# An encoder block on one core: the order of work at the start, and when the first MLP results are squared

## The chip, the cores and the metric

The kernel runs on one core of a Trainium2 chip. Its time is the device time of one execution in microseconds (us). TensorE (PE in the profile) multiplies matrices, VectorE (DVE), ScalarE (ACT) and GpSimd (POOL) do elementwise work, SyncE (SP) issues most DMA transfers. Each engine takes its instructions in the order in which the program lists them.

## The reference, cut to what matters

One layer of an encoder over 1024 tokens of width 1024, everything in float32:

```
u = rms_norm(x, norm1_g);  q,k,v,cb,cc,ch,ga,gb = split(u @ w_in)
y_a = neighbourhood_attention(rms_norm(q), rms_norm(k), v) @ w_attn_branch
y_b = (cb * conv3(cc * ch)) @ w_conv_branch
x = x + (sigmoid(ga) * y_a + sigmoid(gb) * y_b) @ w_o
x = x + square(relu(rms_norm(x, norm2_g) @ w_mlp_in)) @ w_mlp_out
```

## The kernel before, in words

Every float32 operand of a product is scaled by a power of two and split into two float16 halves, high and low: ScalarE writes the high half (a scaled copy), then VectorE the low half (scaled value less high half). A product is three passes over the halves. One call of `unit` is one group of matmuls into one PSUM bank; the work that follows it (`post`) and the background generators (`fg`, `bg`) are advanced by `step` and `tick` behind each unit, and that fixes where their instructions stand in each engine's queue. Nothing is reordered at run time. PSUM has eight banks under three names, d and s with three each, o with two.

**The start.** `ln_step` advances the normalisation of one of eight row blocks of 128 tokens (`norm`): a square with a row sum on ScalarE, five small VectorE steps (`rstd`), then `u` in two halves (L421 on ScalarE, L423 on VectorE). Blocks 0 to 2 are turned by TensorE (`ln_trans`), blocks 3 to 7 by DMA transposes from SP's queue (`ln_turn`, L438) into `uT`. `v_unit` makes V, first in units of 256 columns (blocks 0 to 2, each of the two halves of V's weights), then 512 columns for blocks 3 to 7; then come eight units of Q and eight of K. A weight chunk (`Chunk.prep`) needs a scale for the whole chunk, from a bound on its largest value: V's chunks use the largest absolute value (`largest`, L302 on VectorE), Q, K and others the sum of squares (L241 on ScalarE), summed over the partitions by a matmul with ones (`all_sum`, L179). Then the splits: L291 on ScalarE, L278 on VectorE; for the second piece of each V chunk GpSimd makes the low half (L288 and L276). The weights come by DMA from SP's queue (L210), five pieces ahead.

`sforms` makes sums and differences of row blocks n and n+4 of the normalised `x` for the gates, whose products are later made with seven instead of eight block products: two scaled copies on ScalarE (L475), four additions on GpSimd into a buffer `sform` (L481), a split on ScalarE and VectorE (L483, L485), and a store to DRAM from SP's queue (L490). `SFORM` holds the unit from which each of the four pairs starts. After the fourth Q unit the program needs all four to be stored, since `xt` is given up there.

**The first MLP product.** It has 16 blocks (`quad`) of seven units each. The results of a block lie in a tile `as` with seven slots; two such tiles take turns. `h_done` follows a block: ReLU and square on ScalarE (L1432, L1434, the square also gives the sum from which the next scale comes), four additions (`sums`, L1159, on VectorE for blocks 0 and 1, then on GpSimd), and a store to DRAM (L1438). Blocks 0 and 1 are computed in two halves of 256 columns: 0 first half, 1 first half, 0 second half, 1 second half; after them come whole blocks of 512. Meanwhile the next weights are prepared: row scales (L952), sums of squares (L961), sums of blocks on GpSimd (`tsum`, L966), the column of sums (L932, L933), the matmul with ones, the scale (L182 to L412) and the splits (L981 on ScalarE, L977 on VectorE).

Of the kernel before, what the change touches and what calls it, by code (L numbers as in the profile page):

```python
# [52 lines left out]
def encoder_block(ctx: ExitStack, tc: tile.TileContext, x, weights, cols, gqk, rel, masks, out):  # L53
# [63 lines left out]
    fg, bg = [], []  # L117
# [102 lines left out]
    class Chunk:  # L220


        def __init__(self, kind, widths, tag, rows, half, more):
            self.kind, self.bank = kind, {"V": "o", "Q": "o", "K": "s", "C": "d"}.get(kind)
            self.tag, self.rows, self.widths, self.more = tag, rows, widths, more
            self.offs = []
            self.raw, self.ready, self.half, self.pool = [], more > 0, half, () if half is None else (1,)
            self.split = False

        def prep(self):  # L230
# [4 lines left out]
            tot = sum(k * w for k, w in self.widths)  # L235
            if self.kind in "QKCG":
                self.parts = wsp.tile([128, 2, tot], F16, name="w16_ws", tag="ws")
                for p, (k, w) in enumerate(self.widths):
# [7 lines left out]
                V.tensor_tensor(c, sc[:, a], sc[:, gm2], op=OP.mult)  # L246
                yield from apart(units[0], 2 if self.kind == "Q" else 3)
                yield from all_sum(c, b, bank(self.bank) if self.bank else anybank(), 1e-36)
                yield from pow2_half(b, 14, s, self.inv, more=self.more)
# [19 lines left out]
            prev, scaled = None, {}  # L269
            for it in todo + [None]:  # L270
                if prev:
                    p, parts, f = prev
                    for o, m, c in parts:
                        hi, lo = (self.parts[:, w, f + o:f + o + m] for w in range(2))
                        if p in self.pool:
                            G.tensor_tensor(lo, scaled[p][:, o:o + m], hi, op=OP.subtract)  # L276
                        else:
                            V.scalar_tensor_tensor(lo, self.raw[p][:, o:o + m], sc[:, c:c + 1], hi,  # L278
                                                   op0=OP.mult, op1=OP.subtract)
                    done[0] += 1  # L280
                    load_upto(done[0] + 5)
                splitting[0] = True
                if it:
                    p, parts, f = it
                    if p in self.pool:
                        scaled[p] = w1p.tile([128, 1024], F32, name="scaled", bufs=1)
                        for o, m, c in parts:
                            G.tensor_scalar(scaled[p][:, o:o + m], self.raw[p][:, o:o + m], sc[:, c:c + 1], 1.0,  # L288
                                            op0=OP.mult, op1=OP.mult)
                    for o, m, c in parts:  # L290
                        A.activation(self.parts[:, 0, f + o:f + o + m], self.raw[p][:, o:o + m], AF.Copy,  # L291
                                     scale=sc[:, c:c + 1])
# [172 lines left out]
    turned, formed = [0], [0]  # L465
    SFORM = (6, 8, 10, 12)

    def sforms():

        for n, start in enumerate(SFORM):  # L470
            yield from apart(start, 0)
            assert turned[0] >= n + 5
            z = []
            for b in (n, n + 4):
                A.activation(xt[:, b], xt[:, b], AF.Copy, scale=sc[:, at(ys, b)])  # L475
                z += [xt[:, b, :512], xt[:, b, 512:]]
            f = wqk.tile([128, 4, 512], F32, name="sform", bufs=1)
            v = wqk.tile([128, 4, 2, 512], F16, name="s16", bufs=2)
            for o, a, b, op in ((2, z[0], z[2], OP.subtract), (0, z[2], z[3], OP.subtract),
                                (1, f[:, 0], z[0], OP.subtract), (3, z[1], f[:, 1], OP.add)):  # L480
                G.tensor_tensor(f[:, o], a, b, op=op)  # L481
            yield from apart(start, 2)
            A.activation(v[:, :, 0], f, AF.Copy)  # L483
            yield
            V.tensor_tensor(v[:, :, 1], f, v[:, :, 0], op=OP.subtract)  # L485
            fg.append(sform_store(n, v))

    def sform_store(n, v):
        yield from apart(units[0], 1)
        SP.dma_start(GS[:, n], v)  # L490
        formed[0] = n + 1
# [23 lines left out]
    push(cV[0])  # L515
    ln_step(0, 2)
    tick()
    ln_step(0, 5)
    ln_step(1)
# [10 lines left out]
    tick(1)  # L530
    v_unit(0, 0, 0, 0)
    ln_step(2, 4)
    ln_trans(u16[:, 1], 1, UT)
    ln_step(2, 1)
    tick(3)
    ln_step(2)
    tick(4)
    ln_step(3, 2)
    ln_trans(u16[:, 2], 2, UT)
    ln_step(3, 4)  # L540
    fg.append(qk_gain())
    fg.append(sforms())
    V.tensor_reduce(sc[:, gm2], sc[:, g1], axis=AX, op=OP.max, apply_absolute_value=True)
    mul(gm2, gm2, gm2)
    for p in range(11):
        if p == 3:
            flush()
            push(cQ)
        if 0 < p < 6:
            v_unit(p % 3, p // 3, 1, 2)  # L550
        elif p:
            v_unit(p - 3, None, 2, 4)
        for q in (p,) if p < 6 else (2 * p - 6, 2 * p - 5):
# [5 lines left out]
            if c < 7:  # L559
                ln_step(c + 1, 3)  # L560
    settle()
    flush()
# [48 lines left out]
    for n, (kind, b) in enumerate(todo):  # L611
# [309 lines left out]
    def turn_s(i, f):  # L921
        for n in range(4):
            for s in range(2):
                SP.dma_start_transpose(FORM[f](s)[:, :, 128 * n:128 * n + 128], GS[:, n, i, s])

# [264 lines left out]

    spare = []

# [90 lines left out]
    def forms_m():  # L1283
# [10 lines left out]
        t2 = w4p.tile([128, 2, 512], F16, name="t2", bufs=1)  # L1294
        t4 = w4p.tile([128, 2, 512], F16, name="t4", bufs=1)
        k4 = lambda v: v.rearrange("p (k c) -> p k c", k=4)
        flat = {0: lambda i: P1[0][:, 7, i], 1: lambda i: two[:, 0, i], 2: lambda i: two[:, 1, i],
# [128 lines left out]
    AS, live = {}, set()  # L1426
    bsum, R = [keep(4) for _ in range(4)], [(keep(), keep()) for _ in range(4)]
    r_ready = [False] * 4

    def h_done(q):  # L1430
        f = AS.pop(q)
        A.activation(f[:, 0:4], f[:, 0:4], AF.Relu)  # L1432
        yield
        A.activation(f[:, 0:4], f[:, 0:4], AF.Square, scale=sc[:, c1[q].inv],  # L1434
                     accum_out=sc[:, at(bsum[q // 4], q % 4)])
        yield
        yield from sums(f, G if q > 1 else V)
        SP.dma_start(HS[q // 4][:, :, q % 4], f)  # L1438
# [8 lines left out]
    def quad(q, c0=0, c1=512):  # L1447
# [6 lines left out]
        ps = {}  # L1454
        z = [AS[q][:, i, c0:c1] for i in range(7)]

        def post6(ps):
# [281 lines left out]
```

## Time and profile before

| | us |
|---|---|
| median of 3 runs | 1243.88 (1243.17 to 1244.32) |
| the profiled execution | 1241.45 |
| its span in the profile | 1239.7 |
| TensorE busy | 1200.9 |
| VectorE busy | 930.0 |
| ScalarE busy | 765.2 |
| GpSimd busy | 425.5 |

A row of the order of time gives the start and the duration in us, the engine, the line of the kernel, the operation, the tiles written and read, and in brackets how long the engine was idle before it and what ended that. A row by stage gives the busy time of each engine in that stretch and the granted TensorE clock (1.00 is full).

### The profile page before, as it was taken

The numbers are of one execution on the slowest core, as the hardware profiler recorded it, in microseconds if no ns is written. First come the engines' busy times: TensorE is split into PE (matmuls) and PEld (weight loads), VectorE is DVE, ScalarE is ACT, GpSimd is POOL, SyncE is SP. The second block draws the span as 40 slices with busy tenths as digits, with TensorE's granted clock in tenths as the row PEclk, the third lists the DMA queues.
The fourth block names the chain that finished last, engine by engine and source line by source line (L and its number), as shares of the span: only waits on it lengthen the run. The fifth ranks groups of instructions, "written<-read, shape, count | busy, mean of one in ns | idle before, by whom it ended". The sixth has DMA issues, their size and how long they took to land.

```text
span 1239.7 us, 17066 instructions
## 1 busy us (share of the span) xinstructions
PE 1200.9 (97%) x6294; PEld 575.6 (46%) x6294; DVE 930.0 (75%) x1743; ACT 765.2 (62%) x1179; POOL 425.5 (34%) x289
## 2 busy tenths in 40 slices
PE   5989999999999999999999899999999999999998
PEld 3534444444444444444458344444444444444444
DVE  6668677988557777877877654564546999999997
ACT  6777577787474554536767877877765763645430
POOL 2440003111331111101003356556657473473562
PEclk8999999999999999999999999999999999999999
DMA  6557446656651211216096543553474744436202
GB/s 257 107 203 170 79 120 137 133 119 120 132 144 44 68 45 58 68 34 255 18 178 146 204 150 130 187 171 136 161 288 161 300 167 148 167 116 232 102 34 102
DMA packets 170868, 173.36 MB, mean 140 GB/s; under 512 B 131488, under 2 KB 132000, under 8 KB 166688
## 3 DMA queue, kind: packets, MB, share of 16 engines
q1 hardware_dynamic: 170784, 172.27, 47.0%
q8 instruction: 49, 0.80, 0.3%
q14 instruction: 35, 0.29, 0.1%
HBM read 102.51 MB, written 37.75 MB: 113 GB/s over the span
## 4 chain that ended last, share of the span: by engine, by line
PE 67%; DVE 18%; ACT 7%; issue 4%; DMA 1%; POOL 1%; SPq 0%; DVEq 0%; ACTq 0%; POOLq 0%
PE ps_d L188 26%; PE ps_s L188 20%; PE ps_o L188 18%; PE ps_d L859 3%; DVE sz L797 2%; DVE P L823 2%; DVE w_s L977 2%; DVE w_ws L278 1%; DVE ops L1572 1%; POOL sform L481 1%; DMA raw<-in_weights 1%; ACT w_ws L241 1%; ACT as L1432 1%; DVE sc L302 1%; DVE sg L1093 1%
## 5 line engine op out<-in xcount | busy, mean ns | idle before, releaser
L188 PEld LDWEIGHTS <-ops 128*128 128x128 f16 x1356 | 132.4, 98 | 159.5 <-issue 2.7
L188 PEld LDWEIGHTS <-w 128*128 128x128 f16 x1368 | 133.2, 98 | 145.7 <-issue 7.2
L859 PE MATMUL ps_d<-uT,w_ws 128*128 128x512 f16 x528 | 125.4, 379 | 0.0
L188 PE MATMUL ps_d<-ops 128*128 128x512 f16 (+1 forms) x528 | 118.4, 374 | 0.0
L188 PE MATMUL ps_s<-ops 128*128 128x512 f16 x492 | 113.2, 379 | 1.5 <-DVE ops L1572 1.1
L1563 ACT ACTIVATE ops<-hf,sc 128x2048 f16<-128x2048 f32 x26 | 52.0, 1998 | 93.7 <-PE ps_o L188 34.8
L966 POOL TENSOR_TENSOR tsum<-raw 128x512 f32<-128x512 f32 x28 | 45.5, 1637 | 156.5 <-ACT raw L952 145.8
L188 PEld LDWEIGHTS <-uT 128*128 128x128 f16 x648 | 65.0, 101 | 70.4 <-issue 5.6
L1159 POOL TENSOR_TENSOR as<-as 128x512 f32<-128x512 f32 x56 | 76.6, 1369 | 37.1 <-ACT as L1434 33.8
L188 PEld LDWEIGHTS <-w_s 128*128 128x128 f16 x588 | 56.8, 98 | 69.4 <-DVE w_s L977 1.9
L188 PE MATMUL ps_d<-u2x,w 128*128 128x512 f16 (+1 forms) x360 | 80.0, 372 | 0.0
L1565 DVE SCALAR_TENSOR_TENSOR ops<-hf,sc,ops 128x2048 f16<-128x2048 f32 x26 | 74.2, 2852 | 5.2 <-ACT ops L1563 5.2
L188 PE MATMUL ps_o<-ops 128*128 128x512 f16 x336 | 77.1, 379 | 0.0
L859 PEld LDWEIGHTS <-w_ws 128*128 128x128 f16 x528 | 50.8, 98 | 52.5
L188 PE MATMUL ps_o<-u2T,w 128*128 128x512 f16 (+1 forms) x324 | 71.7, 371 | 0.0
L952 ACT ACTIVATE raw<-raw,sc 128x256 f32<-128x256 f32 x172 | 70.8, 493 | 0.7 <-DMA raw<-in_weights 0.7
L966 POOL TENSOR_TENSOR gsum<-raw 128x512 f32<-128x512 f32 x14 | 18.9, 1371 | 131.7 <-issue 57.1
L981 ACT ACTIVATE w<-raw,sc 128x512 f16<-128x512 f32 (+1 forms) x28 | 24.6, 927 | 61.2 <-DVE sc L411 61.2
L188 PE MATMUL ps_s<-u2T,w 128*128 128x512 f16 (+1 forms) x252 | 54.2, 366 | 2.4 <-DVE as L1467 2.4
L1458 DVE TENSOR_TENSOR as<-ps_d,as 128x512 f32<-128x512 f32 (+1 forms) x15 | 10.1, 673 | 58.8 <-ACT as L1475 58.8
L806 ACT ACTIVATE sz<-sz,sc 128x384 f32<-128x384 f32 (+1 forms) x64 | 37.3, 582 | 26.9 <-DVE sc L797 13.5
L278 DVE SCALAR_TENSOR_TENSOR w_ws<-raw,sc,w_ws 128x512 f16<-128x512 f32 (+2 forms) x72 | 46.1, 690 | 2.4 <-ACT w_ws L291 2.4
(336 smaller groups left out, 2615.2 us busy)
## 6 DMA issues: line engine op xcount, KB each, us to landing
raw<-in_weights SPq DMA_DIRECT2D x89, 512.0 KB, 5.5
hs<-as SPq DMA_DIRECT2D x16, 1792.0 KB, 8.7
hf<-hs SPq DMA_DIRECT2D x26, 1024.0 KB, 6.5
w2x<-in_weights SPq DMA_DIRECT2D x16, 512.0 KB, 8.1
raw<-in_weights SPq DMA_DIRECT2D x16, 384.0 KB, 3.8
xt<-in_x SPq DMA_DIRECT2D x8, 512.0 KB, 9.9
gs<-s SPq DMA_DIRECT2D x4, 1024.0 KB, 6.2
x<-in_x SPq DMA_DIRECT2D x8, 512.0 KB, 10.0
```

The lines of the kernel that those rows point to most:

```text
L188: T.matmul(ps, l, r, start=a, stop=b)
L278: V.scalar_tensor_tensor(lo, self.raw[p][:, o:o + m], sc[:, c:c + 1], hi, op0=OP.mult, op1=OP.subtract)
L797: V.tensor_tensor_reduce(z[:, :d["n"]], d["ps"][:, :d["n"]], bm, sc[:, cneg], 3.0e38, OP.add, OP.min, accum_out=sc[:, d["mx"]])
L806: A.activation(z, z, AF.Exp, scale=-1.0, bias=sc[:, d["mx"]], accum_out=sc[:, d["sm"]])
L823: V.scalar_tensor_tensor(d["lo"], d["z"][:, :d["n"]], sc[:, d["r"]], d["hi"], op0=OP.mult, op1=OP.subtract)
L859: T.matmul(ps, l, r, start=a, stop=b)
L952: A.activation(v, v, AF.Copy, scale=sc[:, at(g, 4 * i + k)])
L966: G.tensor_tensor(t[:, o], a, b, op=OP.add)
L977: V.scalar_tensor_tensor(o(1), w, sc[:, s], o(0), op0=OP.mult, op1=OP.subtract)
L1159: sub.tensor_tensor(z[o], z[a], z[b], op=op)
L1563: A.activation(P[:, 1, 0], hf, AF.Copy, scale=sc[:, Rs])
L1565: V.scalar_tensor_tensor(P[:, 1, 1], hf, sc[:, Rs], P[:, 1, 0], op0=OP.mult, op1=OP.subtract)
```

## The change

At the start:

- Row block 1's scale steps stand ahead of the split of V's first weights, and V's first unit of block 1 stands on TensorE ahead of the transposes of block 2 (before, the other way round).
- V's second weight chunk takes its scale from sums of squares on ScalarE instead of maxima on VectorE. All low halves of V's weights are made by VectorE, none by GpSimd.
- On SP's queue the last two of Q's and K's first weight loads stand ahead of the transpose of block 3; before, that transpose stood between them.
- The gates' sums are made in place in `xt`, and each pair is started and split at its own marks (`SFORM`: mark, pair, 0 for the sums or 1 for the split). The split of the first pair stands behind `u` of block 7 on ScalarE; before it stood ahead. The stores leave from ScalarE's queue. The order of the four sums in DRAM changes, and `turn_s` reads them accordingly.
- Q's weights: their scale and splits are advanced earlier, by more ticks and steps in the loop over V's units. K's weights: six instead of three ticks behind the units 5 to 7 of Q, so scale and splits stand one unit earlier.

In the MLP:

- Block 0's first half is squared and summed by itself, before its second half is computed; its second half and block 1 wait some steps. The four sums of blocks 0 and 1 are issued without steps in between.
- Block 2's slots 4 and 5 for intermediate results lie in two buffers that are free by then (`t2`, `t4`), not in the `as` tile that block 0 still stores from.

```diff
-            if self.kind in "QKCG":
-                self.parts = wsp.tile([128, 2, tot], F16, name="w16_ws", tag="ws")
+            if self.kind in "QKCG" or self.half:
+                self.parts = vhome[0][:, 1] if self.half else wsp.tile([128, 2, tot], F16, name="w16_ws", tag="ws")
...
-                        if p in self.pool:
-                            G.tensor_tensor(lo, scaled[p][:, o:o + m], hi, op=OP.subtract)
-                        else:
-                            V.scalar_tensor_tensor(lo, self.raw[p][:, o:o + m], sc[:, c:c + 1], hi,
-                                                   op0=OP.mult, op1=OP.subtract)
+                        V.scalar_tensor_tensor(lo, self.raw[p][:, o:o + m], sc[:, c:c + 1], hi,
+                                               op0=OP.mult, op1=OP.subtract)
...
-    SFORM = (6, 8, 10, 12)
+    SFORM = ((6, 0, 0), (7, 1, 0), (8, 0, 1), (10, 2, 0), (10, 1, 1), (11, 3, 0), (14, 2, 1), (15, 3, 1))
...
+        for mark, n, split in SFORM:
+            yield from apart(mark, 0)
+            pair = xt[:, n:n + 5:4]
+            if not split:
+                for b in (n, n + 4):
+                    A.activation(xt[:, b], xt[:, b], AF.Copy, scale=sc[:, at(ys, b)])
+                z = [xt[:, b, c:c + 512] for b in (n, n + 4) for c in (0, 512)]
+                for o, a, b, op in ((3, 2, 3, OP.subtract), (2, 0, 2, OP.subtract),
+                                    (0, 3, 0, OP.subtract), (1, 1, 0, OP.add)):
+                    G.tensor_tensor(z[o], z[a], z[b], op=op)
+                continue
...
-        SP.dma_start(GS[:, n], v)
+        A.dma_start(GS[:, n], v)
...
     push(cV[0])
-    ln_step(0, 2)
+    ln_step(0, 7)
     tick()
-    ln_step(0, 5)
...
+    ln_step(1, 4)
+    V.tensor_reduce(sc[:, gm2], sc[:, g1], axis=AX, op=OP.max, apply_absolute_value=True)
+    mul(gm2, gm2, gm2)
     flush()
-    ln_step(1, 5)
+    ln_step(1)
...
-        unit(tok_mms(ps, actU, b, ch, 8, 512, 0), post, 4, 3)
+        unit(tok_mms(ps, actU, b, ch, 8, 512, 0), post, 4, 6 if 4 < n < 8 else 3)
...
-    def h_done(q):
-        f = AS.pop(q)
-        A.activation(f[:, 0:4], f[:, 0:4], AF.Relu)
+    def h_done(q, c0=0, c1=512, wait1=0, wait2=0):
+        f = AS[q] if c1 < 512 else AS.pop(q)
+        v = f[:, :, c0:c1]
+        yield from wait(wait1)
+        A.activation(v[:, 0:4], v[:, 0:4], AF.Relu)
...
+        yield from wait(wait2)
+        if q > 1:
+            yield from sums(v, G)
+        else:
+            for _ in sums(v, V):
+                pass
+        if c1 < 512:
+            return
...
         z = [AS[q][:, i, c0:c1] for i in range(7)]
+        if q == 2:
+            z[4:6] = extra
...
-            if c1 == 512:
-                fg.append(h_done(q))
+            if q == 0:
+                fg.append(h_done(q, c0, c1, 3, 4 if c0 else 24))
+            elif c1 == 512:
+                fg.append(h_done(q, 0, c1, *((2, 6) if q == 1 else ())))
```

More of the change, by code (lines that the diff above doesn't have):

```diff
@@ L226, in __init__ @@
             self.offs = []
-            self.raw, self.ready, self.half, self.pool = [], more > 0, half, () if half is None else (1,)
+            self.raw, self.ready, self.half = [], more > 0, half
             self.split = False
@@ L246, in prep @@
                 V.tensor_tensor(c, sc[:, a], sc[:, gm2], op=OP.mult)
-                yield from apart(units[0], 2 if self.kind == "Q" else 3)
-                yield from all_sum(c, b, bank(self.bank) if self.bank else anybank(), 1e-36)
+                if not self.half:
+                    yield from apart(units[0], 2 if self.kind == "Q" else 3)
+                yield from all_sum(c, b, bank(self.bank) if self.bank else anybank(), 1e-36, not self.half)
                 yield from pow2_half(b, 14, s, self.inv, more=self.more)
@@ L268, in prep @@
                 o += k
-            prev, scaled = None, {}
+            prev = None
             for it in todo + [None]:
@@ L529, in encoder_block @@
     push(cV[1])
-    tick(1)
+    tick(2)
     v_unit(0, 0, 0, 0)
@@ L534, in encoder_block @@
     ln_step(2, 1)
-    tick(3)
+    tick(1)
+    v_unit(1, 0, 0, 0)
+    tick(7)
     ln_step(2)
-    tick(4)
-    ln_step(3, 2)
+    ln_step(3, 1)
     ln_trans(u16[:, 2], 2, UT)
-    ln_step(3, 4)
+    tick(2)
+    ln_step(3, 5)
     fg.append(qk_gain())
     fg.append(sforms())
-    V.tensor_reduce(sc[:, gm2], sc[:, g1], axis=AX, op=OP.max, apply_absolute_value=True)
-    mul(gm2, gm2, gm2)
     for p in range(11):
@@ L548, in encoder_block @@
             push(cQ)
-        if 0 < p < 6:
+        if p == 1:
+            step()
+            tick(2)
+        elif p and p < 6:
             v_unit(p % 3, p // 3, 1, 2)
-        elif p:
-            v_unit(p - 3, None, 2, 4)
+        elif p > 5:
+            v_unit(p - 3, None, 0, 4 if p < 7 else 8)
         for q in (p,) if p < 6 else (2 * p - 6, 2 * p - 5):
@@ L560, in encoder_block @@
                 ln_step(c + 1, 3)
+        if p > 5:
+            step(2)
     settle()
@@ L1189, in encoder_block @@
     PART = ((0, 4), (4, 7))
-    spare = []
+    spare, extra = [], []
     def pieces(n, part):
@@ L1295, in forms_m @@
         t4 = w4p.tile([128, 2, 512], F16, name="t4", bufs=1)
+        extra.extend(t.rearrange("p a c -> p (a c)").bitcast(F32) for t in (t2, t4))
         k4 = lambda v: v.rearrange("p (k c) -> p k c", k=4)
```

36 lines of the change are left out of this document (11 added, 25 removed).

## The prediction

> **What bounds the kernel now.** I read the page first, then busy time by stage, then the order of time in the two stretches that the change touches.
>
> ```profile
> span 1239.7 us, 17066 instructions
> ...
> PE 1200.9 (97%) x6294; PEld 575.6 (46%) x6294; DVE 930.0 (75%) x1743; ACT 765.2 (62%) x1179; POOL 425.5 (34%) x289
> ...
> hs<-as SPq DMA_DIRECT2D x16, 1792.0 KB, 8.7
> ...
> gs<-s SPq DMA_DIRECT2D x4, 1024.0 KB, 6.2
> ```
>
> TensorE is busy 1200.9 of 1239.7 us, so no change that leaves its matmuls alone can bring more than the 38.8 us in which it idles, plus what it runs below full clock. By stage (columns: length, then busy time of PE, PEld, DVE, ACT, POOL, granted clock):
>
> ```profile
> 62.00:79.00 17.00, 11.84 (x53) 5.01 (x53) 12.37 (x14) 14.31 (x18) 7.97 (x6) 1.00 0.50 162
> 79.00:170.00 91.00, 91.00 (x427) 41.46 (x426) 67.65 (x191) 57.49 (x104) 6.86 (x6) 1.00 0.64 150
> ...
> 675.00:700.00 25.00, 20.63 (x125) 12.29 (x124) 14.11 (x31) 18.15 (x26) 7.64 (x6) 0.93 0.35 116
> 700.00:900.00 200.00, 200.00 (x938) 90.73 (x936) 110.18 (x229) 149.57 (x220) 119.67 (x88) 1.00 0.49 162
> ```
>
> Two holes lie inside the change's reach: 5.2 us at 62 to 79 (the last unit of V and the first of Q) and 4.4 us at 675 to 700 (the third unit of the MLP). Behind each TensorE is 100% busy (79 to 170, 700 to 900) while VectorE has 26% and 45% to spare: what is won in either hole is not eaten at once.
>
> The first hole in order of time (start, duration, engine, line, and in brackets the idle time before and what ended it):
>
> ```profile
> 12.78 2.46 DVE L278 SCALAR_TENSOR_TENSOR w_v<-raw,sc,w_v 128x256 f16<-128x256 f32 x4
> 14.29 2.73 POOL L276 TENSOR_TENSOR w_v<-scaled,w_v 128x256 f16<-128x256 f32 x4 [0.15 <-ACT w_v L291]
> ...
> 25.84 4.48 PE L188 MATMUL ps_s<-w_v,uT 128*128 128x256 f16 x24
> 27.93 1.15 ACT L421 ACTIVATE u<-xt,sc 128x1024 f16<-128x1024 f32 x1 [1.04 <-DVE sc L400]
> 29.11 1.28 DVE L423 SCALAR_TENSOR_TENSOR u<-xt,sc,u 128x1024 f16<-128x1024 f32 x1 [0.95 <-ACT u L421]
> 30.42 2.11 SPq L438 DMA_TRANSPOSE uT<-u  x1
> 31.47 1.67 DVE L278 SCALAR_TENSOR_TENSOR w_v<-raw,sc,w_v 128x256 f16<-128x256 f32 x4
> 37.39 1.05 ACT L241 ACTIVATE w_ws<-raw 128x1024 bf16<-128x1024 f32 x1
> 41.17 5.34 PE L188 MATMUL ps_s<-w_v,uT 128*128 128x512 f16 x24
> 57.26 1.13 ACT L421 ACTIVATE u<-xt,sc 128x1024 f16<-128x1024 f32 x1
> 62.09 0.99 SPq L490 DMA_DIRECT2D gs<-s  x1
> 64.43 5.35 PE L188 MATMUL ps_s<-w_v,uT 128*128 128x512 f16 x24 [2.35 <-DMA uT<-u]
> 68.34 2.56 ACT L291 ACTIVATE w_ws<-raw,sc 128x512 f16<-128x512 f32 x4 [0.42 <-DVE sc L253]
> 69.62 0.38 PE L188 MATMUL ps_d<-w_ws,uT 128*128 128x512 f16 x1
> 72.33 5.48 DVE L278 SCALAR_TENSOR_TENSOR w_ws<-raw,sc,w_ws 128x512 f16<-128x512 f32 x6
> 78.30 5.34 PE L188 MATMUL ps_o<-w_ws,uT 128*128 128x512 f16 x24
> 81.81 0.67 ACT L578 ACTIVATE qs<-ps_d,sc 128x512 f32<-128x512 f32 x1
> ...
> DMA to landing us min/median/max: 4.2/4.3/5.5
> ```
>
> The last V unit waits until 64.43 for the DMA transpose of row block 7, whose `u` ScalarE wrote only at 57.26. The first Q unit takes 69.62 to 78.30, 8.7 us for 24 matmuls that need 5.18 (a full unit's 5.34 less the overlap with the next one), since Q's low halves appear one by one beside it.
>
> **The change, part by part.** Start. The first scale still needs its second weight piece by DMA, so TensorE's first product stays where it is. V's first half: eight low halves on VectorE instead of four there and four on POOL. Beside POOL four took 2.46; with POOL idle (31.47) 1.67, 0.42 each. Eight come to 3.3 us behind about 1.1 us of small steps that now go first, done near 17.4 against POOL's 17.02. That is covered: TensorE at half clock needs about as long.
>
> V's second half: its scale comes from two sums of squares on ScalarE (1.17 each in sequence, estimated from the 1.05 row and its read-out) instead of two reductions on VectorE. ScalarE has them by about 21.5, one uT copy behind them by 22.5, and the second product of TensorE, now moved ahead of block 2's transposes, starts there instead of at 25.84. The next starts near 29.4, and V's second half has its eight low halves by 32.05. With three units of 2.6 us the first 512-wide unit could start at 39.8 instead of 41.17.
>
> But the row blocks fall back. Block 3's scale now stands behind those eight splits on VectorE, and on SP's queue its transpose stands behind four weight loads instead of two. Step by step with 1.15 (`u`), 1.28 (its low half), the squares, and the copies of VT between, the transposes leave at about 35.85 (before: 30.42), 39.85, 48.4 (behind Q's four sums of squares on ScalarE), 54.3 and 60.0; block 7's `u` is at 57.5, as the splitting of the gates' sums and its wait for POOL no longer stand ahead of it, which repays the delay. With 4.3 to landing: 40.1, 44.1, 52.7, 58.6, 64.3. The units of 5.18 then start at 40.1, 45.4, 52.7 (a gap of 2.1), 58.6 (0.7) and 64.3 (0.5). So the last V unit starts where it did, and the gain there is 0.1.
>
> Q's scale is then read by VectorE at about 64 and the splits run from 65 (before: 68.34). At 0.69 to 0.91 each (72.33: six in 5.48 beside POOL) the eight low halves are done at 72.5; TensorE, from 69.5 on, wants the last at 74.0. So Q's first unit takes its plain 5.18 and ends at 74.7 instead of 78.46. **Begin: -3.8.** Bounds: +0 (the last transpose 3.8 later) and -5.3 (no gaps; then the low halves at 72.5 hold the unit to 73.1).
>
> The new gap of 2.1 may cost clock. Ahead of 64.43 a gap of 2.35 cost none; ahead of 690.39 (below) one of 2.36 was followed by units of 4.23 and 3.00 where 2.75 is usual, 1.7 lost. If the gap at 52.7 costs that, the units after it run to 64.8 and the sum loses 0.5, since they waited for transposes anyway. [...]
>
> The gates' sums in place (same four POOL adds per pair, no extra buffer), later: covered by the stretch 79 to 170. Stores on ScalarE's queue: SP's issue took 0.99, so four cost ScalarE about 4 us and free SP. By my count Q's first result is read at about 81.8, as before (81.81), now 7.1 us after its unit ends instead of 3.4; with two and three PSUM buffers taking turns, a unit waits only when this exceeds 15.5 (three more units). ScalarE has 33 us to spare up to 170. K's scale in one go: K's splits come one unit earlier in program order; covered.
>
> MLP. The second hole:
>
> ```profile
> 665.05 1.76 ACT L981 ACTIVATE w<-raw,sc 128x512 f16<-128x512 f32 x2 [4.44 <-DVE sc L411]
> ...
> 675.30 1.89 ACT L1432 ACTIVATE as<-as 128x2048 f32<-128x2048 f32 x1
> 677.22 2.00 ACT L1434 ACTIVATE as<-as,sc 128x2048 f32<-128x2048 f32 x1
> 677.42 0.17 PE L179 MATMUL ps_d<-ones 128*128 128x1 bf16 x1
> ...
> 679.23 0.36 ACT L1475 ACTIVATE as<-ps_o 128x256 f32<-128x256 f32 x1
> 679.35 1.42 DVE L1159 TENSOR_TENSOR as<-as 128x512 f32<-128x512 f32 x2 [3.58 <-ACT as L1434]
> ...
> 683.28 1.76 ACT L981 ACTIVATE w<-raw,sc 128x512 f16<-128x512 f32 x2 [3.70 <-DVE sc L411]
> ...
> 686.28 2.47 DVE L977 SCALAR_TENSOR_TENSOR w<-tsum,sc,w 128x1024 f16<-128x1024 f32 x2
> 688.80 1.27 POOL L966 TENSOR_TENSOR tsum<-raw 128x512 f32<-128x512 f32 x1 [10.64 <-DVE w L977]
> 689.91 0.42 DVE L1467 TENSOR_TENSOR as<-ps_s,as 128x256 f32<-128x256 f32 x1
> 690.39 4.23 PE L188 MATMUL ps_s<-u2T,w 128*128 128x512 f16 x12 [2.36 <-DVE as L1467]
> ...
> 694.41 3.00 PE L188 MATMUL ps_d<-u2T,w 128*128 128x512 f16 x12
> 699.21 0.16 DVE L933 CAST ones<-sc 128x1 bf16<-128x1 f32 x1
> 699.42 0.16 PE L179 MATMUL ps_s<-ones 128*128 128x1 bf16 x1 [2.01 <-DVE ones L933]
> ```
>
> ScalarE squares block 0's whole result (1.89 + 2.00) ahead of the copy at 679.23, VectorE's in-order queue waits 3.58 for it, the next weights' scale follows only at 683.28, their low halves end at 688.7, and only then does VectorE read the banks that TensorE wants at 688.0. Now half of those squares run around 661, in the 4.44 us that ScalarE waits ahead of 665.05, and the other half stands behind the copy, which comes at 675.4. The scale is then free at 678.6 (TensorE's column sum is at 677.4), 4.7 earlier. VectorE makes four sums of half length (about 0.4 each, half of 1.42 for two) and the splits by 684.8, and L1467 runs at 686.4, ahead of 687.9: the stall of 2.36 and the cold units (1.7) go. The next column sum needs ScalarE's squares of the weights (688.0) and a copy into a spare buffer, which no longer waits for block 0's store: ready at 689.9, TensorE comes at 693.07. The stall of 2.01 goes too. 699.42 less 693.07: **-6.35.** Bounds: 0 and -6.35.
>
> The store of block 0 is now waited for by VectorE (its first write into the shared slot) at 690.5; it leaves at 680.3 and with 8.7 lands at 689.0. If it is late, the next scale and the sums of block 1 wait behind it, which TensorE feels only some six units on.
>
> Sum: 1241.45 (the profiled execution; span 1239.7) - 10.15 = 1231.3. That execution lies 2.4 under the median; on the median **1233.8**.
>
> **The rivals.** (a) The begin is hidden: the transposes come late enough that Q's first unit ends where it did, 3.7 later than forecast. For it: five transposes move back by up to 5.4. Against it: block 7 catches up. 1243.9 - 6.3 = 1237.6.
>
> (b) The MLP's stall only moves: VectorE's early sums meet POOL's adds (1.27 each). Low halves took 0.62 beside POOL and 0.42 without; L1467 has 1.5 us in hand, gone when two adds stand in the way, and if the stall and its cold clock come back whole 1243.9 - 3.8 = 1240.1. [...]
>
> (c) Slower: a store holds ScalarE's queue until it has landed, 6.2 us each, 24.8 in all. Beyond the 8.4 us in hand (15.5 - 7.1) this is 16.4 us of TensorE: 1233.8 + 16.4 = 1250. It makes the kernel slower from 5.2 us per store on. Against it: SP's row shows 0.99.
>
> **How the numbers follow.** Forecast 0.63, its own range 1231.5 to 1236.3; (a) 0.2; (b) 0.08, of which 0.03 faster by more than 2.5 us; (c) 0.07; no visible change 0.02. The 80% range takes in the forecast, (a), most of (b) and the lower begin bound of -5.3: 1229.5 to 1239.8. A change under 0.2% (2.5 us) is about what a measurement can't tell from none; faster by more 0.86 (0.63 + 0.2 + 0.03), same 0.07, slower 0.07.
>
> **What would show it.** Right: Q's first unit takes about 5.3 us and starts near 69.5; no gap before the third MLP unit nor before the column sum behind it; granted clock 1.00 there. The last V unit waits for uT near 64.3. Wrong: that wait beyond 68, ScalarE idle at its stores, or VectorE's L1467 still later than TensorE.

## The result and the profile after

The changed kernel takes 1235.94 us (1235.42 to 1236.98), the kernel before 1243.45 (1242.72 to 1244.32): a ratio of 0.9939, 95% interval 0.9929 to 0.9949. It is 7.5 us faster. The forecast was 1233.8.

The two profiled executions lie closer together than the medians: 1241.45 and 1236.98, spans 1239.7 and 1235.0. Of those shown, the one before is the lowest and the one after the highest of its kernel; the last section comes back to that. The same four stages as before the change (length, busy time of PE, PEld, DVE, ACT, POOL, granted clock):

```profile
62.00:79.00 17.00, 17.00 (x81) 7.71 (x79) 11.08 (x13) 15.70 (x22) 9.00 (x6) 1.00 0.75 274
79.00:170.00 91.00, 88.80 (x414) 40.03 (x412) 70.06 (x197) 57.78 (x105) 6.77 (x7) 1.00 0.60 132
675.00:700.00 25.00, 25.00 (x139) 13.30 (x137) 18.09 (x35) 22.73 (x36) 8.83 (x7) 1.00 0.46 159
700.00:900.00 200.00, 196.64 (x914) 88.77 (x912) 111.92 (x225) 144.71 (x210) 119.10 (x86) 0.99 0.49 161
```

Both holes are closed. But the two stages behind them, which were 100% busy before, now have holes: 2.2 us and 3.4 us. Of the 2.2 us, 1.34 lie at K's first unit; the rest lies at 157 and 169, around the start of the attention, which now falls into this stage. The order of time shows the first:

```profile
28.73 7.08 PE L188 MATMUL ps_d<-w_v,uT 128*128 128x256 f16 x48 [1.88 <-ACT uT L426]
...
53.64 1.14 ACT L414 ACTIVATE u<-xt,sc 128x1024 f16<-128x1024 f32 x1
...
61.63 5.34 PE L188 MATMUL ps_s<-w_v,uT 128*128 128x512 f16 x24
66.81 5.34 PE L188 MATMUL ps_d<-w_ws,uT 128*128 128x512 f16 x24
71.99 5.34 PE L188 MATMUL ps_o<-w_ws,uT 128*128 128x512 f16 x24
...
105.88 1.06 ACT L598 ACTIVATE q<-qs 128x1024 f16<-128x1024 f32 x1 [2.94 <-DMA qD<-q]
108.09 2.55 ACT L284 ACTIVATE w_ws<-raw,sc 128x512 f16<-128x512 f32 x4
108.84 0.38 PE L188 MATMUL ps_d<-w_ws,uT 128*128 128x512 f16 x1 [0.40 <-ACT w_ws L284]
109.63 2.94 PE L188 MATMUL ps_d<-w_ws,uT 128*128 128x512 f16 x12 [0.41 <-DVE w_ws L276]
113.10 2.58 PE L188 MATMUL ps_d<-w_ws,uT 128*128 128x512 f16 x11 [0.53 <-DVE w_ws L276]
115.52 5.34 PE L188 MATMUL ps_o<-w_ws,uT 128*128 128x512 f16 x24
```

The same two steps before the change, K's splits on ScalarE and the unit behind K's first:

```profile
110.86 2.55 ACT L291 ACTIVATE w_ws<-raw,sc 128x512 f16<-128x512 f32 x4
119.76 5.34 PE L188 MATMUL ps_o<-w_ws,uT 128*128 128x512 f16 x24
```

The last V unit starts at 61.63 with no wait, and the first Q unit ends at 71.99 against 78.30: 6.3 won. Then K's first unit waits for its weights' splits (108.09 on ScalarE, behind the copy of a normalised Q at 105.88), and the unit behind it starts at 115.52 against 119.76: 4.2 are left. By 642 it is 3.5 (the first MLP block starts at 642.28 against 645.75). In the MLP:

```profile
689.67 0.17 PE L179 MATMUL ps_s<-ones 128*128 128x1 bf16 x1
693.10 2.86 DVE L1161 TENSOR_TENSOR as<-as 128x512 f32<-128x512 f32 x4
695.87 2.96 DVE L979 SCALAR_TENSOR_TENSOR w<-raw,sc,w 128x512 f16<-128x512 f32 x2
698.75 4.49 DVE L979 SCALAR_TENSOR_TENSOR w<-tsum,sc,w 128x1024 f16<-128x1024 f32 x2
700.26 4.12 POOL L968 TENSOR_TENSOR tsum<-tsum,raw 128x512 f32<-128x512 f32 x2 [0.31 <-ACT tsum L963]
705.80 1.91 ACT L1439 ACTIVATE as<-as 128x2048 f32<-128x2048 f32 x1 [5.68 <-DVE as L1487]
710.36 0.69 DVE L1474 TENSOR_TENSOR as<-ps_d,as 128x512 f32<-128x512 f32 x1 [4.59 <-ACT as L1493]
711.36 0.16 PE L179 MATMUL ps_s<-ones 128*128 128x1 bf16 x1 [3.36 <-DVE ones L935]
711.38 4.44 PE L188 MATMUL ps_o<-u2T,w 128*128 128x512 f16 x12
```

The same splits and the same column sum before the change:

```profile
702.84 1.94 DVE L977 SCALAR_TENSOR_TENSOR w<-raw,sc,w 128x512 f16<-128x512 f32 x2
704.70 2.47 DVE L977 SCALAR_TENSOR_TENSOR w<-tsum,sc,w 128x1024 f16<-128x1024 f32 x2
715.90 0.16 DVE L933 CAST ones<-sc 128x1 bf16<-128x1 f32 x1
717.57 0.17 PE L179 MATMUL ps_s<-ones 128*128 128x1 bf16 x1
```

The column sum that was at 699.42 comes at 689.67, 9.75 sooner. The next one is 3.36 late, and the unit behind it runs at half clock for a while (4.44 where 2.75 is usual, 1.69 lost; the granted clock is 0.50 from 712 to 715). Block 1's four sums now stand ahead of the weights' splits on VectorE; the splits run beside GpSimd's adds and take 2.96 and 4.49, where the same rows before the change (702.84 and 704.70) took 1.94 and 2.47; ScalarE waits for VectorE, VectorE's next step waits for ScalarE, and the `ones` (the column of sums that VectorE writes for this matmul) come only at 711.1. Of the 9.75 about 4.5 are left at the next column sum, near the difference of the spans (4.7).

### The profile page after: what moved, and what is told of

The parts are those of the page before. It is cut to its first block, busy times and chain, and to the rows that moved or that the text cites. A ratio compares the mean times of both kernels' runs of the same rounds, so it can differ in the third digit from the quotient of the medians.

```text
span 1235.0 us, 17055 instructions
## 1 busy us (share of the span) xinstructions
PE 1198.7 (97%) x6294; PEld 574.6 (47%) x6294; DVE 932.7 (76%) x1754; ACT 768.2 (62%) x1186; POOL 422.5 (34%) x273
## 4 chain that ended last, share of the span: by engine, by line
PE 61%; DVE 22%; ACT 9%; issue 5%; DMA 3%; SPq 0%; ACTq 0%; DVEq 0%
PE ps_d L188 23%; PE ps_s L188 20%; PE ps_o L188 15%; PE ps_d L861 3%; DVE sz L799 2%; DVE P L825 2%; DVE w_s L979 2%; DVE w_ws L276 1%; ACT w_ws L241 1%; DVE ops L1590 1%; DMA qD<-q 1%; DVE w L979 1%; DVE u L416 1%; DVE s L480 1%; DVE sg L1095 1%
## 5 line engine op out<-in xcount | busy, mean ns | idle before, releaser
L188 PE MATMUL ps_s<-u2T,w 128*128 128x512 f16 (+1 forms) x252 | 52.7, 359 | 0.0
L284 ACT ACTIVATE w_ws<-raw,sc 128x512 f16<-128x512 f32 (+2 forms) x72 | 41.3, 639 | 15.6 <-DVE sc L254 15.6
```

Of the source, the lines that this page charges most:

```text
L188: T.matmul(ps, l, r, start=a, stop=b)
```

## The experiments

All ratios are against the kernel before, run on the same chip. Where a run is compared with the changed kernel in us, the medians come from separate measurements on several chips, between which the kernel before itself differed by up to 1.5 us (1243.23 to 1244.71); differences of that size are judged by the ratios and the traces.

**One half at a time.** The begin alone gives the MLP its old `h_done`; the MLP part alone leaves the begin as it was.

```diff
-            if q == 0:
-                fg.append(h_done(q, c0, c1, 3, 4 if c0 else 24))
-            elif c1 == 512:
-                fg.append(h_done(q, 0, c1, *((2, 6) if q == 1 else ())))
+            if c1 == 512:
+                fg.append(h_done(q))
```

> The begin of the change alone; block 1's h is finished as before. Theory (the begin leads by 6.3 at Q's first unit, K's first unit gives 1.9 of it back, and 3.5 are left at 642, which nothing later touches): span 1239.7 - 3.5 = 1236.2, time about 0.9972 of before. The MLP's two stalls (2.4 and 3.6 in before's order) stay. Rival 1 (the MLP's wait takes up a part of the lead, since its column sum hangs on VectorE's and not on TensorE's clock): under 1 us gained, 0.999 or more. Rival 2 (the loss at K's first unit comes from ScalarE's queue as the MLP change moves it): the whole 6.3 stay, 0.995.

Measured: 1238.35 us, 0.9964 (0.9951 to 0.9976), span 1236.2. The first Q unit started at 66.29, the unit behind K's first at 113.93. The theory's 0.9972 is inside the interval, neither rival's figure is (the second's 0.995 only just). In the MLP the two old waits stand:

```profile
685.38 2.75 PE L188 MATMUL ps_s<-u2T,w 128*128 128x512 f16 x12 [2.50 <-DVE as L1470]
694.42 0.16 PE L179 MATMUL ps_s<-ones 128*128 128x1 bf16 x1 [3.69 <-DVE ones L935]
694.44 4.44 PE L188 MATMUL ps_o<-u2T,w 128*128 128x512 f16 x12
```

But that the span is the forecast 1236.2 is luck, since the steps are not the theory's. K's first unit gave back 1.0 and not 1.9 (6.8 sooner at the end of Q's first unit, 5.8 behind K's first), and the first MLP block starts at 640.59, 5.2 sooner than before. Then 1.7 are lost in the MLP, which the theory had untouched: before, the half clock fell ahead of the second wait (a granted clock of 0.50 from 692 to 694) and was taken out of it; here it falls behind it (4.44 where 2.75 is usual, a granted clock of 0.93 over 675 to 700).

> The MLP part alone, with the begin of before. Theory (the first column sum comes 6.28 sooner, and the one after it gives back 3.36 of waiting and 1.69 of half clock, because block 1's sums now stand ahead of the weight splits on VectorE; both hang on VectorE and not on the begin): the span is 1.2 below before's, 0.9990. Rival (the second column sum is late only because the begin has moved the weight loads and GpSimd's adds by 3.5): the 6.3 stay, 0.995. In the trace: theory, VectorE's second weight split of block 3 takes over 4 us and TensorE waits over 3 for the ones; rival, no such wait.

Measured: 1241.03, 0.9982 (0.9974 to 0.9991), span 1237.7, 2.0 below before's. The late column sum is there without the new begin:

```profile
694.09 0.17 PE L179 MATMUL ps_s<-ones 128*128 128x1 bf16 x1
715.78 0.16 PE L179 MATMUL ps_s<-ones 128*128 128x1 bf16 x1 [3.37 <-DVE ones L933]
715.80 2.75 PE L188 MATMUL ps_o<-u2T,w 128*128 128x512 f16 x12
```

So it belongs to the MLP part itself. Here no half clock follows the 3.37 (2.75, a granted clock of 1.00 over 700 to 720). The two halves give 5.15 and 2.47 us of medians, together 7.6; both at once give 7.5.

**Where block 1's sums stand.**

```diff
-                fg.append(h_done(q, 0, c1, *((2, 6) if q == 1 else ())))
+                fg.append(h_done(q, 0, c1, *((2, 12) if q == 1 else ())))
```

> The changed kernel with one number changed: block 1's four sums wait for 12 steps of VectorE's list and not 6, so that they stand behind the weight block's four splits and not ahead of them. Theory (the 2.86 of sums ahead of the splits make them late and push them into GpSimd's adds, and the stall of 3.36 with 1.69 of half clock follows): that stall goes, up to -5.05 against the changed kernel: span about 1230, 0.9900 of before. Rival 1 (the splits are slow because they run beside GpSimd's adds, wherever the sums stand): the splits still take 2.9 and 4.5, at most 2.86 of the wait goes, and 2 us or fewer are won. Rival 2 (TensorE waits for whatever comes last in that chain, and the next column sum, 18 us on, takes it): no gain, 0.994.

Measured: 1237.96, 0.9961 (0.9949 to 0.9974): 2 us or more slower than the changed kernel, worse than any theory had it.

```profile
692.22 1.94 DVE L979 SCALAR_TENSOR_TENSOR w<-raw,sc,w 128x512 f16<-128x512 f32 x2
694.07 2.48 DVE L979 SCALAR_TENSOR_TENSOR w<-tsum,sc,w 128x1024 f16<-128x1024 f32 x2
...
698.39 5.19 DVE L1161 TENSOR_TENSOR as<-as 128x512 f32<-128x512 f32 x4
...
710.55 0.60 ACT L1493 ACTIVATE as<-ps_o 128x512 f32<-128x512 f32 x1 [2.31 <-DMA hs<-as]
...
712.18 0.16 PE L179 MATMUL ps_s<-ones 128*128 128x1 bf16 x1 [5.07 <-DVE ones L935]
```

The splits are on time and fast, as the theory said. But the sums, now beside GpSimd's adds, take 5.19 instead of 2.86 and still stand ahead of VectorE's L1487, for which ScalarE's squares wait; and block 1's store leaves later, so that the next block's first copy waits 2.31 for it. What counts is the whole list up to L1487, not the order inside it.

```diff
-        if q > 1:
+        if q > 0:
             yield from sums(v, G)
```

> The changed kernel with block 1's four sums on GpSimd and not on VectorE. Theory: VectorE's splits start 2.9 sooner and the stall of 3.36 with 1.69 of half clock goes as when the sums are put behind them: span about 1230, 0.9900 of before. Rival (what slows the splits is GpSimd working beside them, and four sums more on GpSimd keep it beside them for longer): the splits take 4 us or more each, and the time is no better than the changed kernel's, 0.994 or above. [...]

Measured: 1231.48, 0.9907 (0.9892 to 0.9923), span 1229.3, 4.5 us faster than the changed kernel (4.0 by the ratios).

```profile
688.56 5.33 POOL L1161 TENSOR_TENSOR as<-as 128x512 f32<-128x512 f32 x4 [1.72 <-ACT as L1441]
692.68 2.94 DVE L979 SCALAR_TENSOR_TENSOR w<-raw,sc,w 128x512 f16<-128x512 f32 x2
695.55 3.49 DVE L979 SCALAR_TENSOR_TENSOR w<-tsum,sc,w 128x1024 f16<-128x1024 f32 x2
...
707.13 0.16 DVE L935 CAST ones<-sc 128x1 bf16<-128x1 f32 x1
707.41 0.17 PE L179 MATMUL ps_s<-ones 128*128 128x1 bf16 x1
```

The splits still meet GpSimd (2.94 and 3.49), but 2.86 of sums have left VectorE's list, and the `ones` are ready just before TensorE wants them. Taking the sums away from VectorE was enough. That GpSimd beside the splits has a share too is read from their durations alone; no run moved GpSimd's adds.

**K's first unit.** First theory: ScalarE's wait for a transpose is to blame.

```diff
-    SFORM = ((6, 0, 0), (7, 1, 0), (8, 0, 1), (10, 2, 0), (10, 1, 1), (11, 3, 0), (14, 2, 1), (15, 3, 1))
+    SFORM = ((6, 0, 0), (7, 1, 0), (8, 0, 1), (10, 2, 0), (10, 1, 1), (11, 3, 0), (12, 2, 1), (13, 3, 1))
```

> The changed kernel with the gates' last two pairs split two units earlier (marks 12 and 13, not 14 and 15). Theory (ScalarE's copy of the first normalised Q waits 2.94 for a transpose that leaves only when the gates' last split has given up its tile; K's splits stand behind that copy, and so the begin gives back 1.9 at K's first unit): the transposes leave sooner, K's splits are in time, and up to 1.9 is won against the changed kernel: span 1233.1, 0.992 of before. Rival 1 (those splits wait for GpSimd's sums in place, wherever they stand; ScalarE and VectorE then hold Q's own work up behind them): K's first unit waits as before and the time is the changed kernel's, 0.994, or above. Rival 2 (the lead is used up before the MLP in any case): K's first unit has no wait and the time is still 0.994.

Measured: 1236.23, 0.9935 (0.9922 to 0.9947), span 1235.3: nothing won, and rival 1 holds.

```profile
84.84 1.91 ACT L478 ACTIVATE s<-xt 128x2048 f16<-128x2048 f32 x1 [1.88 <-POOL xt L473]
...
107.62 2.55 ACT L284 ACTIVATE w_ws<-raw,sc 128x512 f16<-128x512 f32 x4
109.84 2.94 PE L188 MATMUL ps_d<-w_ws,uT 128*128 128x512 f16 x12 [1.08 <-DVE w_ws L276]
```

The wait of 2.94 is gone (0.44 at the same copy, which now starts at 105.42) and K's splits start only 0.5 sooner: the earlier splits of the gates' sums waited for GpSimd (1.88 at 84.84), and Q's own work stands behind them. The theory fell. With block 1's sums on GpSimd besides:

> Block 1's sums on GpSimd, and the gates' last two pairs split two units earlier. Theory (two separate losses, in separate stages): the gains add, 1229.3 - 1.9 = 1227.4 for the span, 0.989 of before. Rival (with the sums on GpSimd the ones came only 0.1 ahead of TensorE; a TensorE that comes 1.9 sooner runs into VectorE's chain there): the 1.9 is lost at the column sum near 705, span 1229.3 or, with half clock behind it, above.

Measured: 1231.57, 0.9898 (0.9885 to 0.9912), as without the earlier splits. Its first Q unit started 1.5 later than with the earlier splits alone, where the program up to there is the same (68.21 against 66.70, after a longer stretch of half clock near 30: 48 matmuls took 8.33 against 7.08, at a granted clock of 0.50 over 28 to 34), and yet the unit behind K's first came no later (115.56 against 115.73). So TensorE's lead does not decide when K starts. That gave the next theory: only the place of K's splits in the list does.

```diff
-                    yield from apart(units[0], 2 if self.kind == "Q" else 3)
+                    yield from apart(units[0], 2 if self.kind in "QK" else 3)
```

> The changed kernel with the column sum for K's scale one unit earlier (two units' distance as for Q, not three), so that six of K's eight splits stand on ScalarE ahead of one more Q block's copy. The split of the gates two units earlier did not help: the wait for the transpose went, but K's splits began at 107.62 instead of 108.09. Theory (what ends K's first unit is the list of Q's own work that stands ahead of K's splits on ScalarE and VectorE; TensorE's lead does not enter it, since in six kernels whose first Q unit starts between 66.29 and 68.21 the unit after K's first starts between 113.93 and 115.87): K's splits begin about 4 sooner, K's first unit takes its plain 5.2, the unit after it starts at 113.5 and not 115.5, and up to 2.0 is won: span 1233.0. Rival (Q's results then stay unread in their banks, and TensorE waits for those instead, before 150 or at the attention that follows): the lead at 642 is the same 3.5, span 1235.

Measured: 1233.45, 0.9927 (0.9913 to 0.994), span 1231.2; 2.5 us faster than the changed kernel by the medians, 1.5 by the ratios, whose intervals overlap. The trace is clearer:

```profile
102.29 3.79 ACT L284 ACTIVATE w_ws<-raw,sc 128x512 f16<-128x512 f32 x6
...
107.30 5.34 PE L188 MATMUL ps_d<-w_ws,uT 128*128 128x512 f16 x24
112.47 5.34 PE L188 MATMUL ps_o<-w_ws,uT 128*128 128x512 f16 x24
```

K's splits begin 5.8 sooner and K's first unit takes its plain 5.2. Of the 3.05 by which the next unit is ahead of 115.52, TensorE had 0.98 already at Q's first unit (65.83 against 66.81), so 2.07 come from here. Both amendments together:

> K's column sum one unit earlier, and block 1's sums on GpSimd. Theory: 1229.3 less up to 2.0, span about 1227.5, 0.989 of before. Rival (a TensorE that comes sooner finds the ones late near 705, where GpSimd's version had 0.1 to spare; or the lead is gone by 642): span 1229.3 or above, 0.990.

Measured: 1228.92, 0.989 (0.9876 to 0.9903), span 1226.8; in the medians the gains add (4.5 and 2.5). This kernel beats both: 14.3 us under the kernel before, 7.0 under the changed one (6.1 by the ratios).

**What in the begin brings the gain.** V's second low halves back on GpSimd:

```diff
+                        if self.half is not None and p == 1:
+                            G.tensor_tensor(lo, scaled[p][:, o:o + m], hi, op=OP.subtract)
+                        else:
```

> The changed kernel with one step of the begin taken back: GpSimd makes the low halves of the second weight piece of each half of V, as before the change. Theory (the begin's gain is that of the order, that is V's second unit and its second scale earlier): the first unit of 512 columns starts within 0.7 of 40.9, Q's first unit ends within 0.7 of 72.0, and the time is within 1 us of the changed kernel's, 0.993 to 0.995. Rival (the gain is that VectorE's first steps no longer run beside GpSimd): Q's first unit ends 2 or more later, time 0.9955 or above.

Measured: 1236.07, 0.9932 (0.9918 to 0.9946); the first 512-wide unit started at 39.32, the first Q unit at 66.71. The start is further from 40.9 than expected, since no half clock fell on the products near 28 here (5.42 for the 7.08 of the changed kernel, a granted clock of 1.00 over 28 to 34); it was lost again in waits of 0.27 and 0.76 for transposes. Q's first unit ended at 71.89, so the rival falls. In time no difference from the changed kernel. The stores back on SP:

```diff
-        A.dma_start(GS[:, n], v)
+        SP.dma_start(GS[:, n], v)
```

> The changed kernel with the four stores of the gates' sums on SP's queue again. Theory (a store costs ScalarE 0.34 to 0.38 for its issue and nothing after, and no engine of the critical path stands behind it): the same time within 0.5 us, 0.9935 to 0.9945. Rival (on SP's queue each store waits for its split, and the transposes of the normalised Q and the loads behind it wait too): K's first unit waits longer than 1.3 and the kernel is 1 to 3 us above the changed one.

Measured: 1237.26, 0.9941 (0.9928 to 0.9953), span 1235.4. K's first unit waited 1.61 against 1.34 in all. The median is 1.3 above the changed kernel's, but the kernel before was 1.3 slower on this chip too (1244.71 against 1243.45); the ratio, 0.9941 against 0.9939, shows no difference. In the changed kernel the issue on ScalarE takes 0.38 and the engine goes on:

```profile
63.01 0.38 ACTq L485 DMA_DIRECT2D gs<-s  x1
```

Then the place of the gates' first split, put ahead of row block 7 by mark 6 in place of 8:

```diff
-    SFORM = ((6, 0, 0), (7, 1, 0), (8, 0, 1), (10, 2, 0), (10, 1, 1), (11, 3, 0), (14, 2, 1), (15, 3, 1))
+    SFORM = ((6, 0, 0), (6, 0, 1), (7, 1, 0), (10, 2, 0), (10, 1, 1), (11, 3, 0), (14, 2, 1), (15, 3, 1))
```

> The changed kernel with the first pair of gates' sums split ahead of row block 7's normalised values, as before the change. Theory (block 7's values come at 53.64 and not 57.26 because ScalarE and VectorE no longer wait there for GpSimd's sums): they come at about 57, the transpose lands near 63.5, the last V unit waits about 2 for it, so that the first Q unit starts near 69 and not 66.8. The time moves less, since K's first unit ends at 115.5 whatever TensorE's lead: within 0.7 us of the changed kernel. Rival (the order of the first scales brings the gain and this does not): block 7's values stay near 54 and the last V unit starts at 61.6. A second rival for the time: the lead lost here is lost for good, and the kernel is 2 above the changed one, 0.9955.

Measured: 1242.22, 0.9995 (0.9986 to 1.0004). With mark 6 the split stands ahead of block 6 as well, one block earlier than before the change. ScalarE waited 5.40 for GpSimd, a V unit 7.22 for its transpose, and the first Q unit started at 75.57. The lead was lost for good, as the second rival had it, and more of it: the median is 6.3 above the changed kernel's, not 2. The place that it had before the change is that of mark 7:

```diff
-    SFORM = ((6, 0, 0), (7, 1, 0), (8, 0, 1), (10, 2, 0), (10, 1, 1), (11, 3, 0), (14, 2, 1), (15, 3, 1))
+    SFORM = ((6, 0, 0), (7, 0, 1), (7, 1, 0), (10, 2, 0), (10, 1, 1), (11, 3, 0), (14, 2, 1), (15, 3, 1))
```

> The changed kernel with the first pair of gates' sums split after row block 6 and ahead of row block 7, where it stood before the change (the run with it ahead of blocks 6 and 7 went one block too far). Theory (that place alone decides when block 7 is ready, since ScalarE waits there for GpSimd's four sums, which end near 53.5): the split takes ScalarE until 55.5, two scaled copies of 2.2 follow, block 7's u comes at 57 to 58 instead of 53.64, the last transpose leaves near 60.5 and lands near 65, and the last V unit starts 3 to 4 later than 61.63. Of this K's first unit gives back the 1.9 that it cost, so the kernel ends 1.5 to 2.5 above the changed one, about 0.9955 of before. Rival (the transposes are spaced by SP and not by u, so that block 7's u has slack): the last V unit starts at 61.6, no change, 0.994.

Measured: 1241.28, 0.9989 (0.998 to 0.9998).

```profile
53.98 1.91 ACT L478 ACTIVATE s<-xt 128x2048 f16<-128x2048 f32 x1 [3.54 <-POOL xt L473]
...
58.35 1.14 ACT L414 ACTIVATE u<-xt,sc 128x1024 f16<-128x1024 f32 x1
66.11 6.72 PE L188 MATMUL ps_s<-w_v,uT 128*128 128x512 f16 x24 [5.07 <-DMA uT<-u]
```

The mechanism is the theory's (block 7 at 58.35, ScalarE waiting for GpSimd); the price was set too low. The last V unit starts 4.5 later and runs partly at half clock (6.72 for 5.34, a granted clock of 0.90 over 62 to 79), and the median is 5.3 above the changed kernel's, not 1.5 to 2.5 (the spans differ by 3.0). So with the split back in this one place the kernel is no faster than with the MLP part alone (1241.03): the other steps of the begin gain nothing without it. Q's first unit still takes its plain 5.2 there, but the last V unit starts 1.7 later than in the kernel before (66.11 against 64.43) and loses 1.4 to half clock, and that eats it. Whether the split's new place would gain as much without the other steps was not tried.

## Why the prediction was right, and where its steps were not

Its time (2.1 too low), its range and its sign held, but errors of opposite sign met in the sum: the begin won 2.5 more than forecast at Q's first unit, and the stages behind the two holes took back 2.1 and 5.05. In the profiled executions the forecast was 1231.3 and the time 1236.98, 5.7 more. The median came 3.5 nearer than that, 3.0 of it because the medians lie further apart than the two profiled executions, which no trace here explains. That the time came so near is luck.

**Begin, forecast -3.8.** The mechanism was right and the term too small: Q's first unit ended 6.3 sooner (71.99), past the lower bound of -5.3. (The 78.46 from which the forecast counts comes from the chain that ended last, where a unit begins when the one before it ends; in the order of time it is 78.30, so the forecast was -3.6.) Q's first unit itself came out as booked, 5.18 for 8.68. What was mis-sized is the start of the last V unit, booked 0.1 sooner and measured 2.8 sooner. The row blocks fell back less than forecast: the first, third, fourth and fifth transpose left at 34.40, 45.62, 50.90 and 57.05, where the forecast had 35.85, 48.4, 54.3 and 60.0, and block 7's `u` came at 53.64 and not at 57.5. I had seen that the gates' split no longer stands ahead of it, but booked it as repaying a delay; the last run shows that with the split put back 5.85 of the 6.3 are gone at the end of Q's first unit (77.84). With the transposes earlier, the gaps of 2.1, 0.7 and 0.5 did not come, and the question whether the gap at 52.7 costs clock did not arise. The sum books nothing for it, and no run shows that a gap of 2.1 costs none: behind the 1.88 near 28 the granted clock over 28 to 34 was 0.72 in the changed kernel and 1.00 with K's column sum moved. "The next starts near 29.4" (28.73) and "the first 512-wide unit could start at 39.8" were near (40.89, with 1.67 of half clock at 28.73, a granted clock of 0.50 from 29 to 32, which no term held). "TensorE at half clock needs about as long" is borne out by the durations and not by the clock on record: behind its first matmul V's first product took 4.59 for 23 (at 14.79; 5.13 at 13.31 before), where later 24 take 2.78 (at 35.65), and the granted clock there reads 1.00 in both traces.

**"K's splits one unit earlier; covered", and "what is won in either hole is not eaten at once".** These failed. A stage in which TensorE is 100% busy says that everyone else was in time for a TensorE of that pace, not by how much. K's splits did begin sooner (108.09 against 110.86 before), but let the unit behind K's first come only 4.2 sooner; TensorE came 6.3 sooner, and 2.1 was lost there. Their start hangs on the list of Q's work on ScalarE and VectorE; only moving them in that list (the column sum one unit earlier) got it back.

**MLP, forecast -6.35.** From the first block's start to the column sum it took 53.67 before (645.75 to 699.42) and 47.39 after (642.28 to 689.67): -6.28. Every wait named there went: neither the third unit of 512 columns (684.50) nor the column sum waits, at a granted clock of 1.00, as the prediction's signs had it. Its third sign, a wait of the last V unit near 64.3, did not come.

**"the sums of block 1 wait behind it, which TensorE feels only some six units on".** This looked at the wrong reason (the store) and took the distance for cover. TensorE felt it one weight block (18 us) on, with 3.36 and 1.69 of half clock: 5.05 of the 6.28. Before, the `ones` of that column sum were ready at 716.06 for 717.57, 1.5 to spare; four sums of 2.86 moved ahead of the splits were more than that, even with no GpSimd beside them. The parts in the experiments agree: the MLP part alone kept 2.5 us of the 6.35.

**Rivals.** (a) did not come: block 7 caught up, by more than thought. (b) had the right mechanism at the wrong block: VectorE meets GpSimd's adds not at L1467 but one weight block later, and there most of the gain was lost. Beside GpSimd's adds the splits took 4.49 for 2.47, and in the run with block 1's sums later the sums took 5.19 for 2.86; how the two engines hold each other up no run shows. (c) is refuted: a store cost ScalarE 0.34 to 0.38.

With the MLP's loss removed (block 1's sums on GpSimd) the span is 1229.3, 10.4 under before. That is near the sum of -10.15, but not by its terms: the holes gave 6.3 and 6.28, and K's first unit still took back about 2. The missing term was what stands behind the holes.

## What to carry to other kernels

A stage where the bottleneck engine is 100% busy has a margin that its busy share does not show; before booking a gain in front of it, read for each operand behind the hole how long it was ready before it was used (1.5 us for the `ones` here). A gain beyond that is lost at that operand, unless the operand comes sooner as well. Work moved forward on an in-order engine is paid by what it now stands ahead of (5.85 us at the end of Q's first unit for the gates' split ahead of block 7): look for the next result that another engine waits for, and compare the moved time with that margin. Giving block 1's sums whole to GpSimd was better here than either place tried for them on VectorE, although VectorE's splits beside GpSimd's work took 2.94 and 3.49 there, for 1.94 and 2.47.

## What the runs showed of the hardware

In these runs the half clock after a gap was not a fixed price of the gap. The same wait of 1.88 (1.87 in the last) near 28 was followed by a stretch of 7.08 in the changed kernel, 8.33 in the kernel with both earlier splits and GpSimd's sums, and 5.41 with K's column sum moved; the granted clock there (28 to 34) was 0.72, 0.50 and 1.00:

```profile
28.00:34.00 6.00, 5.27 (x33) 4.11 (x34) 4.41 (x13) 4.57 (x9) 0.00 (x0) 0.72 0.46 152
```

```profile
28.00:34.00 6.00, 5.12 (x25) 3.54 (x26) 4.41 (x14) 4.57 (x8) 0.00 (x0) 0.50 0.50 165
```

```profile
28.00:34.00 6.00, 5.91 (x55) 5.30 (x55) 4.21 (x13) 4.20 (x11) 0.00 (x0) 1.00 0.56 175
```

These are the changed kernel, the one with both, and the one with K's column sum moved. In the MLP a wait of 3.36 or 3.37 cost 1.69 of clock in the changed kernel and nothing in the MLP part alone. The clearest pair is the last V unit, whose instructions are the same in the kernel before and in the MLP part alone: behind a wait of 2.35 it took 5.35 (the row at 64.43 in the prediction; a granted clock of 1.00 over 62 to 79), behind one of 2.36 it took 7.04 (0.90):

```profile
64.52 7.04 PE L188 MATMUL ps_s<-w_v,uT 128*128 128x512 f16 x24 [2.36 <-DMA uT<-u]
```

What decides between the two these rows do not show. A gap of this length was not safe here: 2.36 was followed by half clock in the row above and in the one at 690.39 before the change (4.23 where 2.75 is usual, a granted clock of 0.50 from 692 to 694). The 1.88 near 28 says less, since it doesn't stand alone: from 24.82 to 28.73 TensorE did only two groups of eight transposes, 1.2 us in all.

What a half-clock stretch cost in the end depended on what followed. Near 28 most of the 1.67 was made up: from 28.73 the changed kernel needs 38.08 to its first Q unit, and the kernel without half clock there (28.09 to 65.83) 37.74, since it then waits for transposes.

The 3 us by which the two profiled executions lie closer together than the medians stay open. Half clock that comes or not would be of that size (two stretches like the 1.67 and 1.69 above, an estimate), but the clocks on record don't bear it out: of the kernel before, on one chip, executions of 1241.19 and 1244.17 both have a mean granted clock of 0.996, while 3 us lost at 0.50, which is 6 of 1240 us, would lower it by about 0.002 (an estimate). At most 0.5 us may lie at the start, which varies by itself: TensorE's first matmul comes at 9.77 before and at 10.32 in the changed kernel's trace, but between 9.62 and 10.43 in the kernels with the same begin up to there. The other executions of these kernels have no trace here.
